# Decoder layer on one core: the modulation computed as rows on the tensor engine, and GpSimd's part of the mixer given to the vector engine

## The chip, the core and the metric

The kernel runs on one core of a Trainium2 chip. The metric is the device time of one execution in microseconds (us). The engines are TensorE (PE, with its weight loads PEld), VectorE (DVE), ScalarE (ACT), GpSimd (POOL) and SyncE (SP, which here issues nearly all loads).

## The reference, cut to what matters

One decoder layer on 256 tokens of width 1024. Six modulation vectors come from one condition vector; a mixer (block attention of 8 heads beside gated linear attention of 4 heads, merged by gates) is followed by a mixture of 32 experts, 4 per token.

```python
c_act = jax.nn.silu(c)                                   # (1, 1024)
mod = (c_act @ w_ada[l] + b_ada[l])[:, None, :]          # (1, 1, 6*1024)
shift1, scale1, gate1, shift2, scale2, gate2 = jnp.split(mod, 6, axis=-1)
h = _rmsnorm(x, norm1_w[l]) * (1.0 + scale1) + shift1
x = x + gate1 * _mixer(h, w_in[l], ...)
h = _rmsnorm(x, norm2_w[l]) * (1.0 + scale2) + shift2
x = x + gate2 * _moe(h, w_router[l], ...)
return _rmsnorm(x, final_norm_w)
```

All arrays are float32. `w_ada` is 1024 x 6144 (25 MB), `w_in` 1024 x 8208, the experts' weights 32 x 12.6 MB, some 403 MB.

## The kernel before, in words

The activations lie transposed: 128 partitions hold channels, the free dimension holds the 256 tokens. A unit is 256 channels, a tile of 128 x 2 x 256.

**Products in the mixer.** A product makes 256 output columns from 1024 inputs in four quarters, one for each unit of the input. Its weights are split into a rounded high part `wh` (`split_hi`, a ScalarE copy, L385) and a low part `wl` (`split_lo`, a subtraction, L389). A quarter is 12 matmuls in which the tile of weights or of activations is loaded and 256 columns stream (`quarter`, L403). Five pairs of split buffers are there. Which engine makes `wl` is written down: quarters 1 and 3 of a product on GpSimd, 0 and 2 on VectorE.

**First block.** The six products that gated linear attention needs first (q, k, half of v) run unit by unit over the input (j = 0 to 3, six quarters each), since a unit of the normalised input `h` exists only when its shift and scale do. `ada_block(j)` loads the two 256-column pieces of `w_ada` for unit j. `ada_steps` accumulates them on VectorE in eight steps of 128 x 512 (L356, L358), `norm_unit` sums over the partitions with four one-column matmuls (L501), adds the bias and makes `h` (L514 to L518).

**Other modulation.** The vectors 2 to 5 (gate1, shift2, scale2, gate2) come from `ada_chain`: eight VectorE steps of 128 x 1024 (L819, L821), two transposes and two sums (L829, L831), a small matmul (L836) and additions (L841). It is a background chain.

**Order.** Engines run their instructions in the order in which they were issued. Products are jobs in a list, and between half quarters `side` lets background chains (levels of the linear attention, its output, gates, rotation, attention heads, modulation) issue a step. It does so by a planner's estimate of each engine's time (`use("V", 0.61)` and the like), with limits on how far an engine may lag. Loads go through a ring of 80 KB per partition in a fixed order; the next load is issued when `used` has been called often enough on the oldest tile.

**Names of the background work.** `level` forms the decays of one distance in linear attention: differences (GpSimd L655, VectorE L656), exponential (L658), products (GpSimd L660, VectorE L661), a matmul (L667, L683). `gla_out` is its output (GpSimd L742 and L758), `rot` the rotation of queries and keys (VectorE L949, L950, GpSimd L952, VectorE L954), `attn` a head of attention (first matmul L893).

**Experts.** After the mixer the 32 experts run one after another; their loads come through the same ring and two more. Their two products stream 512 columns against weight tiles of 64 columns, two side by side (L1328, L1362).

Of the kernel before, what the change touches and what calls it, by code (L numbers as in the profile page):

```python
# [9 lines left out]
F32 = mybir.dt.float32  # L10
# [3 lines left out]
OP = mybir.AluOpType  # L14
# [18 lines left out]
AHEAD, BACKLOG, PLO = 4, 3.0, (1, 3)  # L33
# [13 lines left out]
M_MOD = M_SEG + 64  # L47
M_N = M_MOD + 128
# [10 lines left out]
def constants():  # L59
# [23 lines left out]
    m[:, M_MOD:M_MOD + 128] = (p[:, None] % 32) == (p[None, :] % 32)  # L83
# [20 lines left out]
def layer(ctx, tc, a, out, dbg=None):  # L104
# [51 lines left out]
    modT = const.tile([128, 6, 8], F32, name="modT")  # L156
    bc = [128, 2, NE]
# [15 lines left out]
    with ExitStack() as mx:  # L173
# [85 lines left out]
        def ada_block(j, i):  # L259
# [7 lines left out]
            return queue(emit, 4)  # L267

        def first_block(j, n0, n1):
            def emit():  # L270
                wa = ring.tile([128, 2, 2, 512], F32, name="w")
# [4 lines left out]
            return queue(emit, 2 * (n1 - n0))  # L276
# [3 lines left out]
        la, lw = [], []  # L280
        for j in range(4):
            la.append([ada_block(j, i) for i in range(2)])
            lw.append([first_block(j, 0, 2), first_block(j, 2, 3)])
        l_ada = {v: [] for v in range(2, 6)}

        def ada_loads(v, n):
            for _ in range(n):
                i = len(l_ada[v])
                l_ada[v].append(queue(lambda i=i: wtile(kview(w_ada, D * v, D * v + D, 2 * i, 2 * i + 2)), 2))
# [4 lines left out]
        for v, lst, c0 in ((4, l_gr, C_GR), (3, l_gb, C_GB), (2, l_ga, C_GA)):  # L294
            for i in range(2):
                lst.append(chunk(w_in, c0 + 512 * i))
                if v > 2:
                    ada_loads(v, 2)
        for u in range(4):
# [4 lines left out]
            ada_loads((2, 5)[u // 2], 2)  # L304
# [24 lines left out]
        for u in range(2):  # L329
            V.tensor_mul(sx[u], x0[u], x0[u])  # L330
            S.activation(sx[2 + u], x0[2 + u], AF.Square)
        V.tensor_tensor(sx[0], sx[0], sx[1], op=OP.add)
        V.tensor_mul(cact, cact, vec[:, R_C:R_C + 8])
        V.tensor_tensor(sx[0], sx[0], sx[2], op=OP.add)
# [3 lines left out]
        acc, tpa = {}, [Bank()]  # L338

        def ada_products(k):  # L340

            ld = la[0][k // 4]
            for v in range(2):
                for b in range(2):
                    i = 2 * v + b
                    PE.matmul(tpa[0].t[:, i:i + 1], ld.tv[:, k % 4, v, 128 * b:128 * b + 128], cact[:, k:k + 1],
                              start=(k + i == 0), stop=False, skip_group_check=True)
            ld.used()

        def ada_steps(j, ks, first=True):  # L350
            for k in ks:
# [1168 lines left out]
```

## Time and profile before

| what | value |
|---|---|
| median of 3 runs (lowest to highest) | 1349.86 us (1344.20 to 1350.17) |
| the profiled execution's own time | 1352.94 us |
| its span, first to last instruction | 1351.0 us |
| mean granted clock of TensorE | 0.972 |
| PE, DVE, ACT, POOL busy | 1221.2, 483.6, 290.7, 220.4 us |
| loaded and stored | 480.18 MB |

The span has five stretches, which the program's names mark off: the first block until 82 us; the rest of linear attention and the gates until 210; rotation and attention until 325; the merge and the output product until about 432, where the second expert's matmuls begin to follow each other; then the experts. Busy time of PE is no measure of progress here, since its matmuls overlap: the time from one start to the next is.

### The profile page before, as it was taken

To read this page: it belongs to the slowest core of one execution; us is meant where nothing else is said; L and a number is where in the kernel's file an instruction comes from. 1 tells how busy PE (TensorE), PEld (TensorE's weight loads), DVE (VectorE), ACT (ScalarE), POOL (GpSimd) and SP (SyncE) were. 2 spreads that over 40 slices of the span, in tenths; PEclk is the share of its full clock that TensorE was granted. 3 is DMA by queue.
4 is the path that set the end of the run, shared out by engine and by line. 5 is a ranking of instruction groups with operands and counts; after the bars stand their busy time and mean duration, and the time that the engine had idled before them with its cause. 6 is when DMAs were issued, how large, how long until landed. Compare 5 with 4: busy or idle time off the path is not lost.

```text
span 1351.0 us, 16184 instructions
## 1 busy us (share of the span) xinstructions
PE 1221.2 (90%) x6616; PEld 675.0 (50%) x6616; DVE 483.6 (36%) x800; ACT 290.7 (22%) x597; POOL 220.4 (16%) x153
## 2 busy tenths in 40 slices
PE   6797997879999989999999999898989889898986
PEld 5697997879985434434434333342433334242322
DVE  6749897878533121211221112111111121111112
ACT  3263655445432101101011010110101011010102
POOL 3656574554431000000000000000000000000000
PEclk9799799899999989999999999999999999999998
DMA  8997469567688999999999999999999999999993
GB/s 272 317 285 217 95 150 199 161 177 269 252 310 325 416 414 397 427 427 427 427 427 427 426 426 428 428 426 427 426 428 426 426 426 427 427 427 428 426 426 143
DMA packets 73292, 480.18 MB, mean 355 GB/s; under 512 B 7456, under 2 KB 23984, under 8 KB 48512
## 3 DMA queue, kind: packets, MB, share of 16 engines
q1 hardware_dynamic: 69808, 476.60, 90.2%
q10 hardware_dynamic: 3264, 2.23, 0.5%
q8 instruction: 53, 0.87, 0.3%
q0 software_dynamic: 144, 0.30, 0.1%
q14 instruction: 23, 0.19, 0.0%
HBM read 478.06 MB, written 1.05 MB: 355 GB/s over the span
## 4 chain that ended last, share of the span: by engine, by line
DMA 41%; PE 26%; DVE 1%; issue 0%; ACT 0%; SPq 0%; DVEq 0%; ACTq 0%
DMA w<-in_w_exp_in_dram 26%; DMA w<-in_w_exp_out_dram 15%; PE h L1328 13%; PE g L1362 7%; PE y L1372 2%; PE g L1262 1%; PE g L1352 1%; PE h L1320 1%; PE y L1238 0%; PE h L1218 0%; PE g L1251 0%; DVE o L1424 0%; PE g L1281 0%; DVE u L1366 0%; PE g L1218 0%
## 5 line engine op out<-in xcount | busy, mean ns | idle before, releaser
L1328 PE MATMUL h<-w,xg 128*64 128x512 f32 x2048 | 464.9, 599 | 23.1 <-DMA w<-in_w_exp_in_dram 23.1
L1328 PEld LDWEIGHTS h<-w,xg 128*64 128x64 f32 x2048 | 140.6, 137 | 306.1 <-issue 272.2
L1362 PE MATMUL g<-w,aT 128*64 128x512 f32 x1024 | 230.2, 599 | 28.0 <-DMA w<-in_w_exp_out_dram 14.7
L1341 DVE TENSOR_SCALAR sg<-h 128x512 f32<-128x512 f32 x32 | 22.1, 692 | 524.2 <-PE h L1328 514.3
L403 PE MATMUL ps_a<-m,wh 128*128 128x256 f32 x896 | 176.6, 298 | 3.1 <-ACT m L516 2.0
L389 POOL TENSOR_TENSOR wl<-w,wh 128x512 fp32r<-128x512 f32 x98 | 143.3, 1471 | 110.8 <-ACT wh L385 91.2
L1362 PEld LDWEIGHTS g<-w,aT 128*64 128x64 f32 x1024 | 72.8, 137 | 171.8 <-issue 147.3
L403 PEld LDWEIGHTS ps_a<-m,wh 128*128 128x128 f32 x896 | 148.1, 202 | 4.3 <-ACT m L516 2.1
L403 PE MATMUL ps_a<-m,wl 128*128 128x256 f32 x448 | 131.5, 294 | 12.4 <-DVE wl L389 12.4
L1354 ACT COPY aT<-g 128x512 f32<-128x512 f32 x32 | 18.7, 586 | 509.7 <-PE g L1352 509.7
L385 ACT CAST wh<-w 128x512 fp32r<-128x512 f32 x176 | 106.0, 616 | 97.0 <-PE ps_a L403 70.5
L1366 DVE TENSOR_TENSOR u<-g,u 64x512 f32<-64x512 f32 x64 | 44.0, 688 | 199.4 <-PE g L1362 198.7
L403 PEld LDWEIGHTS ps_a<-m,wl 128*128 128x128 f32 x448 | 90.1, 201 | 13.6 <-DVE wl L389 13.6
L389 DVE TENSOR_TENSOR wl<-w,wh 128x512 fp32r<-128x512 f32 x78 | 75.4, 969 | 23.4 <-ACT wh L385 23.4
L1342 ACT ACTIVATE sg<-sg 128x512 f32<-128x512 f32 x32 | 20.2, 631 | 189.8 <-DVE sg L1341 189.8
L1262 PE MATMUL g<-Psel,u 128*128 128x128 f32 x512 | 60.5, 276 | 0.0
L1372 PE MATMUL y<-u,pT 128*128 128x512 f32 x128 | 59.2, 605 | 0.8 <-DVE u L1366 0.8
L1262 PEld LDWEIGHTS g<-Psel,u 128*128 128x128 f32 x512 | 58.5, 192 | 0.1
L821 DVE SCALAR_TENSOR_TENSOR acc<-w,cact,acc 128x1024 f32<-128x1024 f32 x28 | 44.7, 1597 | 11.5 <-DMA w<-in_w_ada_dram 11.4
L1271 ACT ACTIVATE xg<-xg,shift 128x128 f32<-128x128 f32 x128 | 40.9, 390 | 27.7 <-DVE xg L1268 26.2
L1372 PEld LDWEIGHTS y<-u,pT 128*128 128x128 f32 x128 | 23.0, 189 | 36.8 <-issue 34.6
L403 PE MATMUL ps_a<-u,wh 128*128 128x256 f32 x224 | 40.5, 283 | 0.0
(302 smaller groups left out, 1071.0 us busy)
## 6 DMA issues: line engine op xcount, KB each, us to landing
w<-in_w_exp_in_dram SPq DMA_DIRECT2D x128, 2048.0 KB, 38.8
w<-in_w_exp_out_dram SPq DMA_DIRECT2D x63, 2048.0 KB, 38.1
w<-in_w_in_dram SPq DMA_DIRECT2D x26, 1024.0 KB, 10.4
w<-in_w_ada_dram SPq DMA_DIRECT2D x16, 1024.0 KB, 12.9
w<-in_w_ada_dram SPq DMA_DIRECT2D x32, 256.0 KB, 6.7
w<-in_w_in_dram SPq DMA_DIRECT2D x12, 512.0 KB, 7.3
w<-in_w_o_gla_dram SPq DMA_DIRECT2D x4, 1024.0 KB, 11.7
w<-in_w_o_moba_dram SPq DMA_DIRECT2D x4, 1024.0 KB, 11.7
```

The costliest lines, as they stand in the source:

```text
L385: S.copy(wh, wv)
L389: (G if pool_lo else V).tensor_tensor(wl, wv, wh.bitcast(F32), op=OP.subtract)
L403: PE.matmul(o, lhsT, rhs, start=(b + k + n == 0), stop=(k == 7 and n == 2), skip_group_check=True)
L821: V.scalar_tensor_tensor(acc_, w, ck, acc_, op0=OP.mult, op1=OP.add)
L1262: PE.matmul(o, flat(hx[t, q])[:, 128 * kk:128 * kk + 128], P[:, t], start=(n == 0), stop=(n == 3))
L1271: S.activation(xg[:, kk, 0:w_], xg[:, kk, 0:w_], AF.Identity, bias=shift2[:, kk:kk + 1])
L1328: PE.matmul(ph[64 * hf_:64 * hf_ + 64, 512 * b:512 * b + 512], xg[:, k, SL * i:SL * i + SL], wi[k // 2][:, k % 2, 1024 * hf_ + 512 * b:102 ...
L1341: V.tensor_scalar(sg_, ph[:, 0::2], LIMIT, None, op0=OP.min)
L1342: S.activation(sg_, sg_, AF.Sigmoid, scale=ALPHA)
L1362: PE.matmul(po[64 * n:64 * n + 64, :], aT[:, cc, 64 * hf_:64 * hf_ + 64], wo[hf_][:, cc, 512 * n:512 * n + 512], start=(hf_ + cc == 0), st ...
L1366: V.tensor_mul(flat(og[n])[64 * par:64 * par + 64], po[64 * n:64 * n + 64], flat(g2[n])[64 * n:64 * n + 64])
L1372: PE.matmul(y[t, n], pT[0:rows, 128 * t:128 * t + 128], flat(og[n])[0:rows], start=False, stop=True, skip_group_check=True)
```

## The change

- The modulation is computed on TensorE. The condition vector is the stationary operand, one column of it spread over 32 columns, and 512 columns of `w_ada` stream: `ada_rows(j)` makes 8 such matmuls per unit of the first block, `modulation(v)` 16 for each vector from 2 to 5. Four of them stand in the four 32-column parts of the array and write the four 32-partition parts of a bank. ScalarE copies the bank, and `turn_rows` turns rows into columns with four small matmuls, after which one VectorE addition gives the vector. `ada_steps`, `ada_products` and `ada_chain` are gone.
- `modulation` is a job between products, no background chain; its four loads come together in the ring's order.
- In the mixer all of GpSimd's arithmetic goes to VectorE: `split_lo`, the first halves in `level` (whose two differences become one instruction of 1024 columns, while the exponential becomes two of 512), sums and products in `gla_out`, the rotation, the scaling of x and the sums of squares.
- The sum of squares at the start goes through 16 one-column matmuls instead of VectorE additions and 2.
- The ring's order in the first block interleaves weights and modulation more finely, and the half-used weight tile gets half the room. The planner's prices change (0.53 to 0.63, 0.61 to 0.72, 0.65 to 0.73).

```diff
-        def ada_steps(j, ks, first=True):
-            for k in ks:
-                ld = la[j][k // 4]
-                w, ck = ld.tv[:, k % 4], cact[:, k:k + 1]
-                if first and k == ks[0]:
-                    acc[j] = unit()
-                    V.tensor_scalar(acc[j], w, ck, None, op0=OP.mult)
-                else:
-                    V.scalar_tensor_tensor(acc[j], w, ck, acc[j], op0=OP.mult, op1=OP.add)
-                ld.used()
+        def turn_rows(bk, ev, sel, n):
+            for c in range(4):
+                PE.matmul(bk[:, c:c + 4 * n:4] if n > 1 else bk[:, c:c + 1], ev[:, 128 * c:128 * c + 128], sel,
+                          start=True, stop=True, skip_group_check=True)
+        def ada_rows(j):
+            bk = Bank()
+            for i in range(2):
+                for k in range(4):
+                    PE.matmul(bk.t[32 * k:32 * k + 32, :], cact[:, 4 * i + k:4 * i + k + 1].to_broadcast([128, 32]),
+                              la[j][i].tv[:, k].rearrange("p v n -> p (v n)"), start=(i == 0), stop=(i == 1),
+                              skip_group_check=True)
+                la[j][i].used()
+            ev = unit()[:, :, 0:T].rearrange("p a b -> p (a b)")
+            S.copy(ev, bk.t)
+            return bk, ev
...
-        def split_lo(wv, wh, wl, pool_lo):
-            (G if pool_lo else V).tensor_tensor(wl, wv, wh.bitcast(F32), op=OP.subtract)
+        def split_lo(wv, wh, wl):
+            V.tensor_tensor(wl, wv, wh.bitcast(F32), op=OP.subtract)
...
+                if j < 3 and n == PNORM - 1:
+                    rows = ada_rows(j + 1)
                 if j < 3 and n == PNORM:
-                    norm_unit(j + 1)
+                    norm_unit(j + 1, rows)
...
+        def modulation(v):
+            def f():
+                bk = bank("a")
+                for i, ld in enumerate(l_ada[v]):
+                    for g in range(4):
+                        PE.matmul(bk[32 * g:32 * g + 32, :],
+                                  cact[:, 2 * i + g // 2:2 * i + g // 2 + 1].to_broadcast([128, 32]),
+                                  ld.tv[:, g // 2, 512 * (g % 2):512 * (g % 2) + 512], start=(i == 0), stop=(i == 3),
+                                  skip_group_check=True)
+                    ld.used()
+                ev = late.tile([128, 512], F32, name="ev")
+                S.copy(ev, bk)
...
+                    turn_rows(bk, ev, rows_[:, 1:3], 2)
+                    V.tensor_tensor(modT[:, v], bk[:, 0:8], vec[:, col:col + 8], op=OP.add)
...
-                yield {"V": 1.2}, "G"
-                G.tensor_tensor(sw, sw, sinb, op=OP.mult)
-                yield {"G": 1.25}, "V"
+                yield {"V": 1.4}, "V"
+                V.tensor_mul(sw, sw, sinb)
```

On TensorE at the start of the program the kernel before has this order: products of the condition with the first weights (L346), the sum of squares (L367), its spreading (L372), sums of the VectorE accumulator (L501), then the first quarter.

```order
L346 MATMUL ps_b<-cact,w 128x1 x4
L367 MATMUL y<-ones,u 128x1 x2
L372 MATMUL y<-kt,rs_171 128x128 x2
L346 MATMUL ps_b<-cact,w 128x1 x4
L501 MATMUL ps_b<-ones,u 128x1 x4
L403 MATMUL ps_a<-m,wh 128x256 x2
```

In the changed kernel the same place reads as follows; L353 is `ada_rows`, L345 `turn_rows`, L400 the quarter.

```order
L365 MATMUL ps_b<-ones,u 128x1 x16
L353 MATMUL y<-w,cact 32x512 x8
L371 MATMUL ps_b<-kt,rs_182 128x128 x2
L345 MATMUL y<-rows,u 128x1 x4
L400 MATMUL ps_a<-m,wh 128x256 x2
```

The matmuls with 512 streamed columns have come in ahead of the first quarter, and the sum of squares has grown from 2 to 16 matmuls.

On VectorE in the first block, from making unit 0 of the input (L514, L518) to making unit 1, the kernel before has the eight accumulation steps and no split.

```order
L514 TENSOR_SCALAR u<-u,s_170,modT 128x256 x2
L518 TENSOR_TENSOR m<-u,m 128x256 x2
L356 TENSOR_SCALAR u<-w,cact 128x512
L358 SCALAR_TENSOR_TENSOR u<-w,cact,u 128x512 x7
L504 TENSOR_TENSOR modT<-ps_b,vec 128x2x2
L507 SCALAR_TENSOR_TENSOR s_170<-modT,vec 128x2
```

In the changed kernel the same stretch (units are made by L508 and L512, x is scaled by L580) holds splits.

```order
L508 TENSOR_SCALAR u<-u,s_181,modT 128x256 x2
L512 TENSOR_TENSOR m<-u,m 128x256 x2
L386 TENSOR_TENSOR wl<-w,wh 128x512 x2
L580 TENSOR_TENSOR u<-u 128x512
L386 TENSOR_TENSOR wl<-w,wh 128x512
L498 TENSOR_TENSOR modT<-y,vec 128x2x2
L501 SCALAR_TENSOR_TENSOR s_181<-modT,vec 128x2
```

Eight steps that need the modulation's weights are gone from between the two units, and GpSimd's splits and its scaling of x stand there.

On VectorE in the attention stretch, around the rotation of the third pair of heads' queries, modulation steps (L821) stand between the parts of the rotation in the kernel before.

```order
L821 SCALAR_TENSOR_TENSOR acc<-w,cact,acc 128x1024
L949 STREAM_SHUFFLE rope<-q 32x512
L950 TENSOR_TENSOR q<-q,mt 32x512
L389 TENSOR_TENSOR wl<-w,wh 128x512
L821 SCALAR_TENSOR_TENSOR acc<-w,cact,acc 128x1024
L931 TENSOR_TENSOR u<-y,u 128x256 x2
L821 SCALAR_TENSOR_TENSOR acc<-w,cact,acc 128x1024
L954 TENSOR_TENSOR q<-q,rope 32x512
```

In the changed kernel L927, L928, L930 and L931 are the rotation, all on VectorE.

```order
L927 STREAM_SHUFFLE rope<-q 32x512
L928 TENSOR_TENSOR q<-q,mt 32x512
L386 TENSOR_TENSOR wl<-w,wh 128x512
L930 TENSOR_TENSOR rope<-rope,mt 32x512
L931 TENSOR_TENSOR q<-q,rope 32x512
L909 TENSOR_TENSOR u<-y,u 128x256 x2
```

The modulation steps are gone, and the multiplication that GpSimd made stands one split behind the first half of the rotation.

## Rows read from the trace of the kernel before

**Rows 1.** The page's chain that ended last: shares of the span by engine.

```profile
DMA 41%; PE 26%; DVE 1%; issue 0%; ACT 0%; SPq 0%; DVEq 0%; ACTq 0%
```

**Rows 2.** The same chain in order of time, where it leaves TensorE for the loads: start, length, what.

```profile
719.70 5.33 PE h L1328 x24
725.04 37.95 DMA w<-in_w_exp_in_dram
```

**Rows 3.** Busy time of each engine in the stretches: length, then PE, PEld, DVE, ACT, POOL busy (instructions), granted clock, busy share of the DMA engines, GB/s.

```profile
0.00:82.00 82.00, 59.91 (x365) 55.14 (x366) 52.42 (x71) 27.61 (x48) 42.53 (x34) 0.90 0.97 293
82.00:210.00 128.00, 112.85 (x846) 110.30 (x845) 112.39 (x118) 72.37 (x114) 78.60 (x52) 0.92 0.68 178
210.00:325.00 115.00, 93.74 (x685) 89.29 (x685) 91.85 (x151) 55.40 (x121) 60.42 (x33) 0.93 0.68 179
325.00:432.00 107.00, 103.83 (x784) 89.92 (x783) 49.44 (x104) 44.04 (x87) 38.27 (x34) 0.98 0.79 298
432.00:725.00 293.00, 288.72 (x1351) 113.23 (x1351) 60.35 (x128) 29.32 (x73) 0.57 (x1) 0.99 1.00 421
725.00:1351.00 626.00, 562.16 (x2592) 217.15 (x2592) 117.12 (x233) 61.98 (x156) 0.00 (x0) 0.99 0.97 412
```

**Rows 4.** Who waited for whom on TensorE, in the first three stretches one after another (one row, then four, then three): us in total, times, longest.

```profile
PE ps_b L501 <- DVE u L358: 9.0, 2, 6.3
...
PE ps_a L403 <- DVE wl L389: 5.0, 4, 1.8
PE y L683 <- DVE g L661: 4.3, 1, 4.3
PE y L667 <- DVE g L661: 3.4, 1, 3.4
PE ps_b L683 <- DVE g L661: 1.6, 1, 1.6
...
PE ps_a L403 <- DVE wl L389: 11.7, 4, 5.9
PE y L893 <- DVE k L954: 4.6, 2, 2.6
PE ps_b L893 <- DVE k L954: 3.6, 2, 2.2
```

**Rows 5.** TensorE in order of time in the first block: start, length, operation, the wait before it.

```profile
47.86 1.84 PE L501 MATMUL ps_b<-ones,u 128*128 128x1 f32 x8 [6.32 <-DVE u L358]
49.56 0.77 PE L403 MATMUL y<-wh,m 128*128 128x256 f32 x2
...
50.35 0.63 PE L403 MATMUL y<-wh,m 128*128 128x256 f32 x2
...
50.99 0.63 PE L403 MATMUL y<-wh,m 128*128 128x256 f32 x2
...
54.40 0.40 PE L403 MATMUL ps_a<-m,wh 128*128 128x256 f32 x2
...
54.76 0.40 PE L403 MATMUL ps_a<-m,wh 128*128 128x256 f32 x2
...
65.83 0.77 PE L403 MATMUL y<-wh,m 128*128 128x256 f32 x2
```

**Rows 6.** VectorE, ScalarE and the load queue in order of time in the first block, in that order: the accumulation for unit 3, the wait of a split for its weights, the issue of the last unit's loads.

```profile
52.17 11.81 DVE L358 SCALAR_TENSOR_TENSOR u<-w,cact,u 128x512 f32<-128x512 f32 x7
...
42.81 0.62 ACT L385 CAST wh<-w 128x512 fp32r<-128x512 f32 x1 [6.14 <-DMA w<-in_w_in_dram]
...
38.52 7.29 SPq L264 DMA_DIRECT2D w<-in_w_ada_dram  x8
46.24 1.87 SPq L273 DMA_DIRECT2D w<-in_w_in_dram  x3
```

**Rows 7.** Groups of instructions by line and shape on VectorE and then GpSimd, from 0 to 432 us: busy, mean ns of one, idle time before.

```profile
L389 DVE TENSOR_TENSOR wl<-w,wh 128x512 fp32r<-128x512 f32 x78 | 75.4, 969 | 23.4 <-ACT wh L385 23.4
L821 DVE SCALAR_TENSOR_TENSOR acc<-w,cact,acc 128x1024 f32<-128x1024 f32 x28 | 44.7, 1597 | 11.5 <-DMA w<-in_w_ada_dram 11.4
L358 DVE SCALAR_TENSOR_TENSOR u<-w,cact,u 128x512 f32<-128x512 f32 x26 | 31.3, 1206 | 2.4 <-DMA w<-in_w_ada_dram 1.6
...
L954 DVE TENSOR_TENSOR k<-k,rope 32x512 f32<-32x512 f32 x4 | 9.4, 2353 | 4.1 <-POOL rope L952 4.1
...
L993 DVE TENSOR_TENSOR gt<-ps_a,gt 128x512 f32<-128x512 f32 x4 | 2.8, 692 | 3.3 <-PE ps_a L403 3.3
...
L950 DVE TENSOR_TENSOR q<-q,mt 32x512 f32<-32x512 f32 x4 | 2.7, 679 | 0.1
...
L389 POOL TENSOR_TENSOR wl<-w,wh 128x512 fp32r<-128x512 f32 x98 | 143.3, 1471 | 110.8 <-ACT wh L385 91.2 <-issue 11.9 <-PE ps_a L403 7.1
L952 POOL TENSOR_TENSOR rope<-rope,mt 32x512 f32<-32x512 f32 x8 | 23.4, 2926 | 27.4 <-DVE rope L949 24.7 <-PE ps_a L403 2.7
```

**Rows 8.** VectorE in order of time in the attention stretch, where TensorE's longest wait for a split ends, and once more 56 us later.

```profile
233.33 1.29 DVE L821 SCALAR_TENSOR_TENSOR acc<-w,cact,acc 128x1024 f32<-128x1024 f32 x1 [5.82 <-DMA w<-in_w_ada_dram]
...
235.89 0.67 DVE L389 TENSOR_TENSOR wl<-w,wh 128x512 fp32r<-128x512 f32 x1
...
288.94 1.29 DVE L821 SCALAR_TENSOR_TENSOR acc<-w,cact,acc 128x1024 f32<-128x1024 f32 x1 [5.62 <-DMA w<-in_w_ada_dram]
```

**Rows 9.** TensorE in order of time among the first experts: tiles of 64 columns (L1328), transposes at the full array (L1352), full-width rows of 512 columns (L1238).

```profile
435.48 8.80 PE L1328 MATMUL h<-w,xg 128*64 128x512 f32 x40
444.21 0.75 PE L1352 MATMUL g<-kt,li 128*128 128x128 f32 x4
444.89 5.37 PE L1328 MATMUL h<-w,xg 128*64 128x512 f32 x24
...
461.74 3.70 PE L1238 MATMUL y<-u,wT 32*128 32x512 f32 x8
465.37 0.72 PE L1320 MATMUL h<-bx,sel 128*128 128x512 f32 x2
```

More of the change, by code (lines that the diff above doesn't have):

```diff
@@ L156, in layer @@
     modT = const.tile([128, 6, 8], F32, name="modT")
+    rows_ = const.tile([128, 3], F32, name="rows")
+    V.memset(rows_, 0.0)
+    for g in range(4):
+        V.memset(rows_[32 * g:32 * g + 1, 0:1], 1.0)
+        V.memset(rows_[32 * g:32 * g + 1, 1 + g % 2:2 + g % 2], 1.0)
     bc = [128, 2, NE]
@@ L266, in emit @@
                 return wa
-            return queue(emit, 4)
+            return queue(emit, 1)
         def first_block(j, n0, n1):
             def emit():
-                wa = ring.tile([128, 2, 2, 512], F32, name="w")
+                wa = ring.tile([128, n1 - n0, 2, 512], F32, name="w")
                 for n in range(n0, n1):
@@ L275, in emit, with ada_loads @@
                 return wa
-            return queue(emit, 2 * (n1 - n0))
+            return queue(emit, 2 * (n1 - n0), 4 * KB * (n1 - n0))
         blocks = [(C_GQ + 256 * u, False) for u in range(4)] + [(C_GV + 256 * u, True) for u in range(2)]
         nb_ = len(blocks)
-        la, lw = [], []
+        la, lw = [[ada_block(0, i) for i in range(2)]], []
         for j in range(4):
[L282 to L289, printed above, removed]
+            lw.append([first_block(j, 0, 2)])
+            if j < 3:
+                la.append([ada_block(j + 1, i) for i in range(2)])
+            lw[j].append(first_block(j, 2, 3))
+        l_ada = {}
+        def ada_loads(v):
+            l_ada[v] = [queue(lambda i=i: wtile(kview(w_ada, D * v, D * v + D, 2 * i, 2 * i + 2)), 1)
+                        for i in range(4)]
         l_gr, l_gb, l_ga, l_qk, l_v, l_og, l_om, l_ow = [], [], [], {}, {}, [], [], []
@@ L361, in layer @@
-        pn_ = Bank()
-        ada_products(0)
-        ada_steps(0, [1])
-        V.tensor_tensor(sx[0], sx[0], sx[3], op=OP.add)
-        V.tensor_tensor(sx[0][:, 0], sx[0][:, 0], sx[0][:, 1], op=OP.add)
-        for t in range(2):
-            PE.matmul(pn_.t[:, t:t + 1], sx[0][:, 0, 128 * t:128 * t + 128], ones[:, 0:1], start=True, stop=True)
+        def turn_rows(bk, ev, sel, n):
+            for c in range(4):
+                PE.matmul(bk[:, c:c + 4 * n:4] if n > 1 else bk[:, c:c + 1], ev[:, 128 * c:128 * c + 128], sel,
+                          start=True, stop=True, skip_group_check=True)
@@ L368, in layer @@
+        pn_ = Bank()
+        for u in range(4):
+            for b in range(2):
+                for t in range(2):
+                    PE.matmul(pn_.t[:, t:t + 1], sx[u][:, b, 128 * t:128 * t + 128], ones[:, 0:1],
+                              start=(u + b + t == 0), stop=(u + b == 4), skip_group_check=True)
         S.activation(rs1, pn_.t[:, 0:2], AF.Sqrt, bias=epst, scale=1.0 / D)
-        ada_steps(0, [3, 4], False)
+        rows0 = ada_rows(0)
         V.reciprocal(rs1, rs1)
@@ L494, in go, with norm_unit @@
             settle(True)
-        def norm_unit(j):
-            tp = Bank() if j else tpa[0]
-            for i in range(4):
-                cs = slice(128 * i, 128 * i + 128)
-                PE.matmul(tp.t[:, i:i + 1], flat(acc[j])[:, cs], ones[:, 0:1], start=(j + i > 0 and j > 0), stop=True,
-                          skip_group_check=True)
+        def norm_unit(j, rows):
+            tp, ev = rows
+            turn_rows(tp.t, ev, rows_[:, 0:1], 1)
             js = slice(2 * j, 2 * j + 2)
```

150 lines of the change are left out of this document (52 added, 98 removed).

## Prediction, made before the changed kernel ran

> **What bounds the kernel now.** I read the chain that ended last first [rows 1], then its order in time [rows 2]: from 725 us on it consists of expert loads alone, before that of the experts' matmuls. Then the stretches [rows 3]. From 432 us on the loads run at 421 and 412 GB/s with their engines 97 to 100% busy; the experts cannot run faster than that, whatever the mixer does. Before 432 us the loads run at 178 to 298 GB/s; they wait for room in the ring. So the span is the mixer's length plus a stretch that the loads fix, and a microsecond saved before 432 us is a microsecond at the end. I take that transfer as 1 to 1: the loads' shares from 432 us on (1.00, 0.97) leave nothing to be filled or lost there.
>
> What bounds the mixer? TensorE. A quarter's three matmuls take 0.36 us from start to start at the full clock (54.40 to 54.76) and 0.64 us at half of it (50.35 to 50.99) [rows 5]. The mixer has 38 products and the first block's 6, 176 quarters by the splits' counts, 78 on VectorE and 98 on GpSimd [rows 7], each of 12 matmuls: 176 x 4 x 0.36 = 253 us of 432. The rest is smaller matmuls, waits, and time at 1.2 instead of 2.4 GHz. Who ends the waits stands in [rows 4]; what the clock costs follows from the granted clock of a stretch [rows 3], since half the clock shows there as a loss of half the time: (1 - 0.90) x 82 = 8.2 us in the first, 0.08 x 128 = 10.2, 0.07 x 115 = 8.1 and 0.02 x 107 = 2.1 us. The engine had waited before these stretches (6.32 us ahead of 47.86, and the quarters after it run at the slow pace [rows 5]).
>
> **The price of the new matmuls.** No 32-column tile is in the trace. The nearest row is the experts' 64-column tiles: 40 records from 435.48 to 444.21, 0.218 us each [rows 9]. A full-width row of 512 columns costs 0.454 us per record (8 in 3.63 us) [rows 9]; two tiles side by side thus cost half of one. Each float32 matmul is two records (32 matmuls of an expert are the 64 records 40 + 24). If four tiles run beside each other as two do, a record is 0.109 us. The change has 4 x 8 + 4 x 16 = 96 such matmuls, 192 records: 21 us at 0.109, 42 us at 0.218, 87 us at 0.454. I take 0.109, since the step that the rows show, from one tile to two, is a clean halving; the other two are rivals. Turning rows into columns is 8 small records, 0.9 us at full clock by half of what L501's 8 cost at the slow one (1.70 us, 47.86 to 49.56 [rows 5]); in the first block they replace L501, behind it they are new.
>
> In the experts, four transposes between two runs of 64-column tiles take 0.68 us from first start to the next tile's (444.21 to 444.89), 0.17 us each [rows 9]; that is all a change of tile shape and back shows. The Trainium skill (TensorEngine Tiling (Array Packing), Tiling Modes, Key Properties) says that changing the tiling mode drains the engine. By that rule each of 16 changes would cost about 0.36 us (the last of 24 records takes 5.37 - 23 x 0.218 from its start to its end), an estimate of 6 us; but two changes and four transposes together take only 0.68 us here, so the trace shows no such cost, and the sum goes without it.
>
> **First block, 0 to 82 us.** Removed: TensorE's wait for the accumulation, 9.0 us [rows 4], and most of the slow clock that followed it, 6 of 8.2 us. Added: the rows of units 1 to 3, 16 records each, 3 x 1.75 = 5.2 us; at the start about 2 us, since the sum of squares is 28 records more at 0.21 us (6 us, half of it while x still arrives), and unit 0's rows go ahead of the first quarter while four splits stand on VectorE ahead of the unit's making. The floor is the loads: unit 3's modulation weights are issued until 45.8 us and the last weights until 48.1 [rows 6], with the engines' share at 0.97 [rows 3]; unit 2's split waited 6.14 us for its weights [rows 6]. Landing near 53 us puts unit 3's first quarter no earlier than about 57, against 65.83 now [rows 5]. So the block can give 9 + 2 = 11 us at most; by the engine's own sum 15 - 5.2 - 2 = 8. I take **-6.5 us** (-11 to 0), since the next block's loads begin no earlier.
>
> **Linear attention and gates, 82 to 210 us.** Waits: 5.0 us for splits, 9.3 for `level`'s products [rows 4], clock 10.2. VectorE is busy 112.4 of 128 us [rows 3], so its queue is long. Of it 24.9 us or more go with the modulation (28 steps of 1.6 us [rows 7], half of them here). Splits shrink from 0.97 us to the 0.69 that the same shape costs where GpSimd rests (L993) [rows 7], and all come to VectorE. I let 3.5 us of the splits' waits, 5 of `level`'s (its chain stays: difference, exponential, product) and 6 of the clock go: -14.5. Added: two modulations, 2 x (16 x 2 x 0.109 + 0.9) = 8.8. **-6 us** (-16 to +4).
>
> **Attention, 210 to 325 us.** Two waits of the splits are not VectorE's work but its queue: a modulation step stood 5.82 and 5.62 us for its weights [rows 8] with splits behind it; that is most of the 11.7 us [rows 4], and 10 of it go. The rotation runs VectorE, GpSimd, VectorE; GpSimd's part is 2.93 us and the addition behind it up to 2.35 [rows 7], against 0.68 each for the same shape uncontended (L950) [rows 7]. That is some 3 us less in each of 8 chains, and of the 8.2 us that TensorE waited for it [rows 4] 6 go. Of the clock's 8.1, 6 go. Added: two modulations, 8.8, less about 0.8 for the small matmuls dropped. **-14 us** (-20 to -4).
>
> **Merge, 325 to 432 us.** TensorE is busy 103.8 of 107 [rows 3]; GpSimd's splits here were ahead of need. **-1 us** (-4 to +1).
>
> **VectorE as a whole.** 306 us are busy before 432 [rows 3]. Gone: 76 us in L821 and L358 alone [rows 7]. Splits: 176 x 0.692 = 122 instead of 75.4, +46. GpSimd's others: 24 tiles of 512 columns (scaling, products, rotation, normalisation) at 0.69, 17 us, and a few small ones. Contention saves about 12 on L954 and its like. That is about 285 of some 405 us, 70% as now (306 of 432, 71%). On average it keeps up.
>
> **Sum.** -6.5 - 6 - 14 - 1 = -27.5 us. The profiled execution took 1352.94 us (its span 1351.0 and 1.9 around it), so it would be 1325.4; the median of the runs lies 3.1 us lower, at 1349.86, so the forecast is **1322 us**.
>
> **Rivals.**
> 1. *Nothing is left of the waits and the slow clock.* All lower ends: -51 us, 1299. For it: VectorE loses a fifth of its work at the crowded place, and a wait avoided also avoids the slow clock. Against: `level`'s chain of four engines stays.
> 2. *Tiles run in pairs only*, 0.218 us per record: +21 us, 1343.
> 3. *VectorE's order is the bound.* It now makes every split in program order, among `level`'s and the rotation's instructions; TensorE would wait for splits as now. Then only the first block (-6.5) and the two waits on modulation loads with their clock (-9.7 - 4) are won, and 16.8 us of modulation added behind the first block: -3.5, so 1346. For it: 88% busy from 82 to 210 us [rows 3]. Against: each split is a third shorter.
> 4. *Slower: the 32-column tiles run one after another*, each at the price of a full-width row, 0.454 us: 87 instead of 21 us, +66, so 1388. It decides from (27.5 + 21) / 192 = 0.25 us per record: above that the change loses. Against it: the 64-column tiles overlap.
>
> **How the numbers follow.** Chances: forecast 0.60 with a range of its own of 1306 to 1338, rival 1 0.10, rival 2 0.12, rival 3 0.12, rival 4 0.06. A measurement of this kernel tells about 0.5% (6.7 us, 1343.1 and 1356.6) from no change. Faster: 0.60 + 0.10 + half of rival 2 (0.06) + a little of rival 3 (0.02) = 0.78; same: 0.06 + 0.08 = 0.14; slower: rival 4 and a tail of rival 3, 0.08. The range goes from just below rival 1 to rivals 2 and 3, **1297 to 1345**; it leaves out rival 4, half of rival 3 and the far tail.
>
> **What would show it.** In the changed profile: records of the 32-column tiles about 0.11 us apart (L353, L809), 3.5 us per modulation; L389's successor L386 at about 0.69 us; unit 3's first quarter at 57 to 62 us; waits of TensorE before 432 us down from 54 us behind the start to some 25; granted clock of 0.95 or more from 82 to 325 us; the second expert's matmuls beginning near 405 us; loads saturated behind that as now. Wrong would be it if TensorE waits for splits by more than 15 us in all, if a modulation takes 7 us or more, if the first block still ends near 80 us because its loads come no earlier, or if the modulation job waits for its four loads.

## The result, and the profile after

The changed kernel takes **1300.54 us** (median of 4 runs, 1297.8 to 1304.11) against 1350.01 (4 runs of the kernel before): ratio 0.9644, 95% interval 0.9604 to 0.9684. The forecast was 1322, range 1297 to 1345. The profiled execution took 1304.11 us, its span is 1302.3.

Line numbers shift: the rows of the modulation are made in L353 (first block) and L809, turned into columns in L345; a split's low half is L386, the product of a quarter L400, a level's product L677, the rotation L927 to L932, the scores L871.

The stretches (the first four cuts at the same places of the program as in [rows 3], the last again where the chain that ended last leaves TensorE for the loads; length, PE, PEld, DVE, ACT, POOL busy with instructions, granted clock, DMA share, GB/s):

```profile
0.00:74.00 74.00, 64.67 (x442) 54.46 (x443) 29.61 (x73) 29.20 (x52) 2.27 (x6) 1.00 0.96 303
74.00:188.00 114.00, 113.38 (x936) 106.35 (x938) 85.60 (x137) 71.71 (x123) 0.00 (x0) 1.00 0.79 231
188.00:283.00 95.00, 94.24 (x767) 87.47 (x760) 70.20 (x155) 58.32 (x130) 0.00 (x0) 1.00 0.80 224
283.00:389.00 106.00, 102.79 (x766) 89.03 (x764) 58.59 (x126) 42.13 (x80) 4.81 (x6) 0.97 0.72 275
389.00:703.00 314.00, 309.77 (x1456) 122.86 (x1458) 66.38 (x141) 33.05 (x84) 0.57 (x1) 0.98 0.99 421
703.00:1302.30 599.30, 541.01 (x2490) 207.67 (x2486) 110.94 (x220) 58.30 (x145) 0.00 (x0) 0.99 0.97 415
```

From 74 to 283 us TensorE is busy for all but 1.4 us, at a granted clock of 1.00 where [rows 3] had 0.92 and 0.93. VectorE took over GpSimd's work and is nevertheless less busy: 244 us up to 389 instead of 306 up to 432. All that TensorE waited for from 30 to 389 us, to be laid beside [rows 4] (us in total, times, longest; the rows with 0.4 us or less left out):

```profile
PE ps_a L1145 <- DVE msk L1142: 1.3, 1, 1.3
PE ps_a L1013 <- DVE lbase L1010: 1.1, 1, 1.1
PE ps_a L345 <- ACT ev L815: 0.7, 1, 0.7
PE ps_a L400 <- DVE wl L386: 0.6, 1, 0.6
PE ps_a L1117 <- ACT m L1067: 0.5, 1, 0.5
```

The first two and the last are the router's and were there before. Of the waits for splits one of 0.6 us is left, those for the levels and for the rotation are gone, and from 74 to 283 us the granted clock is 1.00. The price of the new matmuls, TensorE in order of time: the turning of unit 3's rows with the quarter behind it, unit 3's own first quarter, and a whole modulation between two quarters.

```profile
59.04 0.95 PE L345 MATMUL y<-rows,u 128*128 128x1 f32 x8
59.84 0.48 PE L400 MATMUL y<-wh,m 128*128 128x256 f32 x2
...
62.80 0.40 PE L400 MATMUL ps_a<-m,wh 128*128 128x256 f32 x2
...
187.45 0.28 PE L400 MATMUL ps_a<-m,wl 128*128 128x256 f32 x1
187.66 3.64 PE L809 MATMUL ps_a<-w,cact 128*32 128x512 f32 x32
191.23 0.51 PE L400 MATMUL ps_a<-m,wh 128*128 128x256 f32 x2
```

From the first of the 32 records to the next quarter 3.57 us pass, 0.112 us per record; the change of tile shape and back is within that. Groups by line and shape, to be laid beside [rows 7]:

```profile
L386 DVE TENSOR_TENSOR wl<-w,wh 128x512 fp32r<-128x512 f32 x176 | 115.5, 684 | 38.6 <-ACT wh L382 37.9
...
L656 DVE TENSOR_TENSOR g<-g,gq 128x512 f32<-128x512 f32 x8 | 5.5, 685 | 0.0
L930 DVE TENSOR_TENSOR rope<-rope,mt 32x512 f32<-32x512 f32 x8 | 5.4, 672 | 0.0
```

The chain that ended last is as before [rows 1], loads and the experts' matmuls:

```profile
DMA 42%; PE 27%; DVE 1%; issue 0%; ACT 0%; SPq 0%; DVEq 0%; ACTq 0%
```

Where the 48.7 us between the two spans came from, by the same instruction in both traces: unit 3's first quarter 71.02 to 62.80 us (8.2); the last gate's activation 211.7 to 188.1 (15.4 more); the first product with `gt` 329.9 to 284.9 (21.4 more); the second expert's matmuls 435.5 to 392.4 (1.9 given back); the end (5.6 more). So 43 us come up to the second expert and 5.6 from the experts' stretch, which the forecast had left alone.

### The profile page after: what moved, and what is told of

The parts are those of the page before. It is cut to its first block, busy times and chain, and to the rows that moved or that the text cites. A ratio compares the mean times of both kernels' runs of the same rounds, so it can differ in the third digit from the quotient of the medians.

```text
span 1302.3 us, 16455 instructions
## 1 busy us (share of the span) xinstructions
PE 1225.9 (94%) x6844; PEld 667.8 (51%) x6844; DVE 421.3 (32%) x847; ACT 292.7 (22%) x612; POOL 7.6 (1%) x13
## 3 DMA queue, kind: packets, MB, share of 16 engines
HBM read 477.99 MB, written 1.05 MB: 368 GB/s over the span
## 4 chain that ended last, share of the span: by engine, by line
DMA 42%; PE 27%; DVE 1%; issue 0%; ACT 0%; SPq 0%; DVEq 0%; ACTq 0%
DMA w<-in_w_exp_in_dram 27%; DMA w<-in_w_exp_out_dram 15%; PE h L1305 14%; PE g L1339 7%; PE y L1349 2%; PE g L1239 2%; PE g L1329 1%; PE h L1297 1%; PE y L1215 0%; PE g L1228 0%; PE h L1195 0%; DVE o L1401 0%; PE g L1258 0%; DVE u L1343 0%; PE g L1195 0%
## 5 line engine op out<-in xcount | busy, mean ns | idle before, releaser
L400 PE MATMUL ps_a<-m,wh 128*128 128x256 f32 x896 | 172.0, 293 | 3.8 <-ACT m L510 3.8
L400 PEld LDWEIGHTS ps_a<-m,wh 128*128 128x128 f32 x896 | 144.0, 197 | 6.8 <-ACT m L510 3.8
L400 PE MATMUL ps_a<-m,wl 128*128 128x256 f32 x448 | 129.2, 288 | 0.6 <-DVE wl L386 0.6
L386 DVE TENSOR_TENSOR wl<-w,wh 128x512 fp32r<-128x512 f32 x176 | 115.5, 684 | 38.6 <-ACT wh L382 37.9
L400 PEld LDWEIGHTS ps_a<-m,wl 128*128 128x128 f32 x448 | 88.2, 197 | 0.8 <-DVE wl L386 0.8
L400 PE MATMUL ps_a<-u,wh 128*128 128x256 f32 x224 | 40.7, 283 | 0.0
L400 PE MATMUL ps_a<-wh,m 128*128 128x256 f32 x192 | 34.9, 284 | 0.0
L400 PEld LDWEIGHTS ps_a<-u,wh 128*128 128x128 f32 x224 | 34.4, 189 | 0.0
## 6 DMA issues: line engine op xcount, KB each, us to landing
w<-in_w_in_dram SPq DMA_DIRECT2D x26, 1024.0 KB, 14.3
```

The costliest lines, as they stand in the source:

```text
L386: V.tensor_tensor(wl, wv, wh.bitcast(F32), op=OP.subtract)
L400: PE.matmul(o, lhsT, rhs, start=(b + k + n == 0), stop=(k == 7 and n == 2), skip_group_check=True)
```

## The experiments

Two theories at the start. **Queue**: the gain comes from the modulation's leaving VectorE's order, where its steps stood for their loads with splits behind them [rows 8]. **Port**: it comes from GpSimd's leaving, since VectorE and GpSimd slow each other [rows 7]. All times below are medians; the kernel before took 1350.1 to 1350.3 beside these runs. Two smaller parts of the change, the finer order of the loads in the first block and the sum of squares on TensorE, were never run by themselves; every variant of the changed kernel keeps them. The places are starts in each run's trace: the last gate's activation, the first product with `gt`, the last merged unit `x1T`, the second expert.

| kernel | us | ratio to before (95%) | gate | gt | x1T | expert 2 |
|---|---|---|---|---|---|---|
| before | 1350.0 | | 211.7 | 329.9 | 404.1 | 435.5 |
| changed | 1300.5 | 0.9604 to 0.9684 | 188.1 | 284.9 | 361.0 | 392.4 |
| GpSimd back | 1324.3 | 0.9754 to 0.9850 | 199.6 | 304.8 | 377.5 | 413.6 |
| before, GpSimd moved | 1335.8 | 0.9842 to 0.9936 | 192.5 | 310.4 | 384.9 | 420.9 |
| tiles one by one | 1324.4 | 0.9755 to 0.9853 | 198.4 | 305.7 | 378.9 | 415.0 |
| GpSimd beside splits | 1368.7 | 1.0092 to 1.0185 | 214.7 | 338.9 | 428.7 | 464.7 |
| GpSimd on its own tile | 1306.3 | 0.9631 to 0.9715 | 191.6 | 289.2 | 363.2 | 399.3 |
| VectorE's time back | 1310.9 | 0.9669 to 0.9755 | 187.6 | 286.3 | 365.0 | 396.3 |
| GpSimd moved, waits only | 1319.0 | 0.9726 to 0.9826 | 184.5 | 295.4 | 369.9 | 401.2 |
| before, 32 bytes | 1340.7 | 0.9904 to 0.9985 | 204.8 | 323.3 | 397.5 | 428.9 |
| splits back | 1302.6 | 0.9627 to 0.9698 | 188.1 | 287.1 | 360.3 | 391.7 |
| chains back | 1313.8 | 0.9703 to 0.9775 | 196.7 | 293.5 | 369.6 | 400.9 |
| changed, aligned | 1298.3 | 0.9592 to 0.9648 | 187.9 | 284.8 | 360.8 | 392.2 |

**GpSimd back.** The changed kernel with GpSimd's part of the mixer returned to it:

```diff
-            V.tensor_tensor(wl, wv, wh.bitcast(F32), op=OP.subtract)
+            (G if pool_lo else V).tensor_tensor(wl, wv, wh.bitcast(F32), op=OP.subtract)
...
-                V.tensor_mul(sw, sw, sinb)
+                G.tensor_tensor(sw, sw, sinb, op=OP.mult)
```

> The changed kernel with all of GpSimd's work in the mixer put back on GpSimd (low halves of quarters 1 and 3, the normed units, two steps of each level of linear attention, the halves' sums, gv's scaling, the sine product of the rotation), with the planner's old prices for it; the modulation stays on TensorE. Queue theory (the gain comes from the modulation's leaving VectorE's in-order queue): at most 10 us over the changed kernel's 1300.5, about 1305, PE's idle time before 389 us still under 25 us. Port theory (the gain comes from GpSimd's leaving, since VectorE and GpSimd slow each other): most of the 49 us is gone, 1335 or more, and VectorE's splits cost 0.97 us again instead of 0.68.

1324.3, in the gap: 23.8 us lost where the queue theory allowed 10 and the port theory wanted 35. VectorE's splits took 0.86 us, not the 0.97 of the port theory. TensorE's waits there:

```profile
PE y L871 <- DVE k L932: 4.7, 3, 2.1
PE y L677 <- DVE g L655: 3.6, 4, 1.4
PE y L661 <- DVE g L655: 2.7, 1, 2.7
```

They are at the scores and at the levels, none at a split. Neither half of the change is enough.

**Before, GpSimd moved.** The kernel before with `V.` for `G.` at GpSimd's instructions of the mixer, same places, same prices.

> The kernel before with all of GpSimd's instructions in the mixer issued on VectorE at the same places of the program; the modulation stays on VectorE, the planner's prices stay. Queue theory: VectorE keeps the modulation's waits and gets 116 us more beside it, so that nothing is won: 1345 to 1365. Port theory: splits at about 0.69 us and no detours over a second engine, about 1310 to 1320.

1335.8, between the two ranges again: 14.3 us won beside 1350.1, so the port theory's half exists, but by itself it is the smaller one. At the last `x1T` the two halves win 26.6 (404.1 to 377.5) and 19.2 us (404.1 to 384.9), together 45.8, and the whole change 43.1: nearly the same sum, but not by adding up place by place. In the first block either half wins all there is (the first copy of `gv` starts at 70.4 and 70.8 us, 71.3 in the changed kernel, 79.6 before), and GpSimd moved does so without the new order of the loads; behind it the halves win 17.4 and 10.4 us, the whole 34.8. There each half leaves waits that the other would have removed (12.3 us at the levels and the scores with GpSimd back, 21.9 us for splits here).

**Tiles one by one.**

```diff
-                for i, ld in enumerate(l_ada[v]):
-                    for g in range(4):
+                for g in range(4):
+                    for i, ld in enumerate(l_ada[v]):
```

> The changed kernel with the modulation's matmuls reordered so that those of one tile of 32 columns follow each other (two in a row in the first block's row, four in a row for the later quarters), and not one of each tile in turn. If the four tiles work side by side and TensorE sets the mixer's pace: a record costs up to the 0.454 us of a full matmul instead of 0.118, 192 of them add up to 64 us, 1330 to 1365. If the low price comes from the 32 columns alone and not from neighbours in other tiles: 1300 to 1305.

1324.4, between the two ranges. TensorE in order of time in this kernel: a row of the first block and the quarter behind it, then a modulation of 32 records and the quarter behind it. Below that, weight loads of the same modulation, of which each record has one at its start:

```profile
55.49 1.94 PE L353 MATMUL y<-w,cact 128*32 128x512 f32 x16
57.36 0.50 PE L401 MATMUL y<-m,wh 128*128 128x256 f32 x2
...
159.85 8.86 PE L810 MATMUL ps_a<-w,cact 128*32 128x512 f32 x32
168.64 0.51 PE L401 MATMUL ps_a<-m,wh 128*128 128x256 f32 x2
```
```profile
160.30 0.11 PEld L810 LDWEIGHTS ps_a<-w,cact 128*32 128x32 f32 x1 [0.32 <-issue]
160.73 0.11 PEld L810 LDWEIGHTS ps_a<-w,cact 128*32 128x32 f32 x1 [0.32 <-issue]
161.16 0.11 PEld L810 LDWEIGHTS ps_a<-w,cact 128*32 128x32 f32 x1 [0.32 <-issue]
```

From the first record of the modulation to the quarter 8.79 us pass, 0.275 us per record instead of 0.112: the low price does come from the neighbours in the other tiles. The 0.275 is a mean of two kinds. The first records follow each other at 0.43 us, nearly the 0.454 of a full row [rows 9]; later, 12 of the 32 start within 0.03 us of the one before them (the trace doesn't name a record's tile). In the first block, where only two matmuls in a row go to one tile, nothing is lost: 1.87 us for 16 records, 0.117 each. 128 x (0.275 - 0.112) = 21 us of TensorE's time more make the first product with `gt` 20.8 us later and `x1T` 17.9; the missing 3 us are the slow clock of the changed kernel there (granted 0.97 from 283 on, 0.03 x 106 = 3.2), which doesn't occur in this run ahead of `x1T` (1.00). So TensorE's time is the mixer's time, nearly 1 to 1.

**GpSimd beside splits, and on its own tile.** Useless GpSimd work in the changed kernel, first on the split's halves, then on a private tile:

```diff
             V.tensor_tensor(wl, wv, wh.bitcast(F32), op=OP.subtract)
+            for b in range(2):
+                G.tensor_tensor(gd, wl[:, b].bitcast(F32), wh[:, b].bitcast(F32), op=OP.subtract)
```
```diff
             V.tensor_tensor(wl, wv, wh.bitcast(F32), op=OP.subtract)
+            G.tensor_copy(gs, wl[:, 0, 0:1].bitcast(F32))
+            G.tensor_tensor(gd, gd, gd, op=OP.subtract)
```

> The changed kernel with useless work on GpSimd beside each split: two subtractions of 128x256 that read the split's halves and write a tile that nobody reads (about 176 x 1.6 us of GpSimd); nothing waits for them but the split buffer's next use. Port theory: VectorE's splits go back to about 0.97 us and the time rises by 15 us or more, to 1315 to 1335. Queue theory: splits may get dearer, but VectorE is only 60 per cent busy, so the time rises by at most 5 us, to 1300 to 1306.

> The changed kernel with useless work on GpSimd beside each split that touches a tile of its own (one subtraction of 128x256 on a private tile, behind a copy of one column of the split's low half, which sets its moment): about 176 x 1.1 us, as much GpSimd time as the variant with GpSimd's work put back had (200 us). Nothing of the kernel's work runs on GpSimd. Theory that VectorE and GpSimd slow each other: the splits rise from 0.68 to 0.85 us or more, and the time rises by 8 to 25 us, to 1309 to 1325. Theory that GpSimd's own slowness on the path is what costs (its splits of 1.4 us, the hops to it and back): splits may rise, but the time stays within 5 us, 1298 to 1306.

The first came out at 1368.7, far above what either theory gave, and doesn't separate them. The splits rose to 1.01 us as the port theory wanted, but GpSimd was so slow (two times 0.97 us) that ScalarE stood for split buffers which GpSimd still read (who waited for whom on ScalarE):

```profile
ACT wh L382 <- POOL gd L390: 86.4, 65, 3.2
```

In the second nothing waits so. VectorE's and GpSimd's groups:

```profile
L390 DVE TENSOR_TENSOR wl<-w,wh 128x512 fp32r<-128x512 f32 x176 | 125.2, 741 | 31.8 <-ACT wh L382 22.2 <-POOL gd L392 4.5 <-DMA w<-in_w_ada_dram 3.5
...
L392 POOL TENSOR_TENSOR gd<-gd 128x256 f32<-128x256 f32 x176 | 138.5, 787 | 0.0
```

The splits rise only to 0.74 us, and the last `x1T` comes 2.2 us later. The time, 1306.3, is 5.8 us above the changed kernel's; the two intervals overlap, though no run of the one lies within the runs of the other, and in the profiled execution 4.7 us of the difference fall behind `x1T` (the last section). Slowing VectorE's splits by a tenth costs little, then; but the load on it was also weaker than in the kernel before, where a split took 0.97 us. The next two runs settle this.

**Splits back, chains back.** The two kinds of GpSimd's work returned one at a time, with the lines of the first diff above.

> The changed kernel with only the splits' low halves put back on GpSimd (quarters 1 and 3 of each product, and all but one in the first block), at the planner's old prices; the chains (levels of linear attention, sums, gv's scaling, rotation) stay on VectorE. Of the 16.5 us that the whole of GpSimd's work put back cost up to the end of the mixer (last x1T at 377.5 us instead of 361.0): theory that the splits on GpSimd are what costs, 10 us or more here, 1311 or more. Theory that the chains on GpSimd cost (each level and each rotation waits for a slower step there): at most 5 us here, 1298 to 1307.

> The changed kernel with only the chains put back on GpSimd (two steps of each level of linear attention, the halves' sums, gv's scaling, the sine product of the rotation, the normed units), the splits all on VectorE. Theory of the chains: 10 us or more, 1311 or more, with PE's waits at the levels' matmuls and at the scores as in the run with all of it put back. Theory of the splits: at most 5 us, 1298 to 1307.

With the splits back (groups on VectorE and GpSimd):

```profile
L386 DVE TENSOR_TENSOR wl<-w,wh 128x512 fp32r<-128x512 f32 x78 | 66.4, 853 | 31.5 <-ACT wh L382 31.5
...
L386 POOL TENSOR_TENSOR wl<-w,wh 128x512 fp32r<-128x512 f32 x98 | 136.9, 1402 | 212.7 <-ACT wh L382 191.7 <-PE ps_a L400 13.9 <-DVE sm L888 3.4
```

VectorE's splits are slowed to 0.85 us, GpSimd's take 1.40, and nothing is lost: 1302.6, `x1T` at 360.3. The splits stand four quarters ahead of their use. With the chains back it is 1313.8, `x1T` 8.6 us later: TensorE waits at the levels again (4.1 us), and its first quarter starts at 25.7 instead of 22.7 us. The first four splits on VectorE, which stand ahead of the making of unit 0, show why; first in the changed kernel, then with the chains back, where GpSimd scales x at the same time:

```profile
19.21 2.50 DVE L386 TENSOR_TENSOR wl<-w,wh 128x512 fp32r<-128x512 f32 x4 [0.66 <-ACT wh L382]
```
```profile
17.73 5.82 POOL L580 TENSOR_TENSOR u<-u 128x512 f32<-128x512 f32 x4 [14.41 <-ACT u L374]
18.99 5.71 DVE L386 TENSOR_TENSOR wl<-w,wh 128x512 fp32r<-128x512 f32 x4 [5.86 <-ACT wh L382]
```

Three of the splits take 1.74 to 1.77 us beside GpSimd, and the fourth 0.68 once GpSimd is done. So the port theory falls as it was put: the engines do slow each other, but for the splits that stand ahead of their use it costs nothing. It costs where the slowed step stands in a chain that TensorE waits for, as here at the start (3.0 of the 8.6 us). Both kinds back cost 16.5 at `x1T`, more than 8.6: VectorE's product in the levels takes 1.45 us there and 1.05 with the chains alone. How much of that difference is the slowing and how much GpSimd's own order, where a chain's step then stands among splits of 1.4 us, no run separates.

The Trainium skill (SBUF — State Buffer, Terms) says that VectorE and GpSimd share a port pair that one of them holds for a whole instruction while the other stands. The durations agree in direction: 0.68 to 0.85 us in the mean for a split beside 98 GpSimd instructions of 1.4 us, and 1.74 to 1.77 us for the three splits above.

**VectorE's time back, and GpSimd moved with waits only.** What of the modulation's steps was the cost on VectorE? The first adds their time without their loads to the changed kernel, the second takes their time out of "before, GpSimd moved" and leaves their waits (four of the six modulation vectors come out incomplete in it, so the experts' work behind them can differ):

```diff
+                        V.scalar_tensor_tensor(acc_, acc_, cact[:, i:i + 1], acc_, op0=OP.mult, op1=OP.add)
+                    yield {"V": 1.2}, ""
```
```diff
-                    V.scalar_tensor_tensor(acc_, w, ck, acc_, op0=OP.mult, op1=OP.add)
+                    V.scalar_tensor_tensor(acc_[:, 0:1], w[:, 0:1], ck, acc_[:, 0:1], op0=OP.mult, op1=OP.add)
```

> The changed kernel with as much useless work on VectorE as the modulation's steps of the later quarters were (28 steps of 128x1024 and 16 of 128x512 on a private tile, put in line by the planner at the old price), without any wait for a load. Theory that VectorE's time was the cost of the modulation there: the time rises by 12 us or more, to 1312 to 1325. Theory that the steps' waits for their loads, with the splits behind them, were the cost: at most 5 us more, 1298 to 1306.

> The kernel before with GpSimd's instructions on VectorE, as in the run before, but 28 of the 32 steps of the later quarters' modulation take one column instead of 1024 (so four of the six modulation quarters come out incomplete): each still waits for its load in VectorE's queue, at the same place, and costs next to nothing else. Theory that VectorE's time was the cost: 10 to 25 us under the 1336 of the run with the whole steps, 1311 to 1326. Theory that the waits for loads were the cost: within 6 us of it, 1330 to 1338.

The first gave 1310.9 (`x1T` 4.0 us later), between the two bounds: VectorE's time alone costs something, but less than the theory of time said (part of it may be the order, since the planner places what it prices). The second gave 1319.0, 16.8 us under the whole steps, as that theory said; 15.0 of it are there at `x1T`, ahead of the choice of experts. So the steps' time weighs most where waits stand in the same queue; that a wait leaves a backlog which long steps prolong is my reading of the two, not measured by itself. What the waits do by themselves is seen in this second run, VectorE and then TensorE in order of time:

```profile
195.61 0.67 DVE L389 TENSOR_TENSOR wl<-w,wh 128x512 fp32r<-128x512 f32 x1
207.74 0.22 DVE L821 SCALAR_TENSOR_TENSOR acc<-w,cact,acc 128x1 f32<-128x1 f32 x1 [11.46 <-DMA w<-in_w_ada_dram]
207.88 0.69 DVE L389 TENSOR_TENSOR wl<-w,wh 128x512 fp32r<-128x512 f32 x1
```
```profile
208.62 0.58 PE L403 MATMUL ps_a<-wl,m 128*128 128x256 f32 x1 [7.28 <-DVE wl L389]
209.00 0.63 PE L403 MATMUL ps_a<-wh,m 128*128 128x256 f32 x2
```

A step of one column waits 11.46 us for its load; the split behind it is next; TensorE stands 7.28 us for that split and then goes on at half pace (0.64 us from 209.00 to the next three matmuls at 209.64, against 0.36 [rows 5]). All its waits for splits there sum to 19.0 us. In the changed kernel no matmul waits for these loads: TensorE is idle for 0.0 us ahead of L809.

**Before, 32 bytes; changed, aligned.** The 5.6 us of the experts' stretch: the landings of the experts' loads (2 MB each) follow each other in 4.90 us (median for each of nine buffers, 600 to 1250 us) before, and after in 4.84 to 4.85 for the five buffers of the first ring, 4.88 for one and 4.90 for three. The change adds a small tile (`rows`) ahead of that ring, so its start moves by 32 bytes (as reckoned from the sizes of the tiles, from 32 short of a multiple of 4096 onto one; no trace shows an address). The three at 4.90 are those of a ring allocated from the other end, which did not move.

```diff
     modT = const.tile([128, 6, 8], F32, name="modT")
+    pad = const.tile([128, 8], F32, name="pad")
+    V.memset(pad, 0.0)
```

> The kernel before with an unused tile of 32 bytes a partition among the constants, so that the ring that the experts' loads land in starts at the same place as in the changed kernel (a multiple of 4096 bytes instead of 32 bytes short of one); nothing else changes. If the place in memory explains that the experts' loads of 2 MB land every 4.84 us instead of every 4.90 in the changed kernel, in those buffers that moved and in no other: the same here, 430 GB/s instead of 427 in the experts' stretch, and 3 to 6 us less than before, about 1345. If the rate comes from anything else in the change: 427 GB/s and 1350.

> The changed kernel with two unused tiles (480 bytes at the far edge, 128 bytes in the experts' pool), which move the four of the nine buffers of the experts' loads that don't lie on a multiple of 512 bytes onto one; nothing else changes. If the place sets the rate: all nine at 4.84 us per load instead of 4.88 to 4.90 in those four, 434 GB/s instead of 430, and 190 loads bring 4 to 5 us, about 1296. Otherwise 430 GB/s and 1300.5.

The experts' stretch (columns as above) of before, before with 32 bytes, changed, changed and aligned:

```profile
600.00:1250.00 650.00, 604.68 (x2808) 232.82 (x2808) 122.00 (x247) 60.68 (x155) 0.00 (x0) 1.00 1.01 427
```
```profile
600.00:1250.00 650.00, 611.14 (x2848) 237.22 (x2849) 124.20 (x252) 63.82 (x163) 0.00 (x0) 0.99 1.01 430
```
```profile
600.00:1250.00 650.00, 604.38 (x2812) 232.12 (x2813) 123.95 (x248) 61.87 (x156) 0.00 (x0) 1.00 1.01 430
```
```profile
600.00:1250.00 650.00, 605.80 (x2813) 233.09 (x2810) 123.93 (x248) 61.27 (x155) 0.00 (x0) 1.00 1.01 430
```

The unused 32 bytes alone bring 430 GB/s and 1340.7 us (0.9904 to 0.9985 of before). Of its 9.6 us some 6 are the rate, 0.7% of the 919 us behind 432 us in which the loads bound [rows 3]; the rest isn't explained by it, as its mixer also ran 6.6 us shorter in the one trace, and runs of the kernel before spread over 14 us. All traces agree on the direction: from the second expert to the end the three kernels with the old place (before; GpSimd moved; waits only) take 913 to 916 us, the ten with the new one 903 to 910. The second kernel did not do what I expected: all nine buffers now land every 4.85 us, but the rate stays at 430, and 1298.3 can't be told from 1300.5. It is the lowest median of all, and no proven gain. In its one trace the stretch from the second expert to the end is 6.7 us shorter than in the changed kernel's (903.3 against 909.9), but the rate between 600 and 1250 us doesn't show from where. What the last buffers bring stays open.

## Why the prediction was right, and where its sizes were off

The direction, the bound and the mechanism were right; the forecast was 21 us too high, and the time is close to rival 1 (1299).

1. *TensorE sets the mixer's time, 1 to 1*: right, by the tiles one by one (21 us more of TensorE's time, 20.8 us later at the first product with `gt`).
2. *0.109 us per record of a 32-column tile*: 0.112. Turning took 0.95 us, as forecast. Rival 2 (0.218) and rival 4 (0.454) fall. A record with none beside it does cost nearly what rival 4 said (0.43 in the tiles one by one), but even that kernel won (1324.4): the 128 records of its later modulations take 0.275 in the mean and the first block's 0.117, some 0.23 together, just under the 0.25 from which rival 4 saw a loss. That point also hung on the gain, which I had too small.
3. *Changes of tile shape cost nothing*: right, 3.57 us for 32 records with both changes in it. By the Trainium skill's rule (TensorEngine Tiling (Array Packing), Tiling Modes, Key Properties: a change of mode drains the engine) the estimate was 6 us in all; the trace doesn't show it.
4. *First block, -6.5*: -8.2, within its bounds. The row at 65.83 us [rows 5] that I took for unit 3's first quarter is unit 2's fifth; it is at 59.84 now, within the 57 to 62 named. Unit 3's own went from 71.02 to 62.80. The start cost more than the 2 us of the sum: the first quarter begins at 22.7 instead of 19.2 us.
5. *Linear attention and gates, -6*: **-15.4**. The term that failed is what I kept of the waits: 1.5 us of the splits', 4.3 of `level`'s ("its chain stays"), 4.2 of the clock's, 10 us in all. All of it went but 0.6 us. The chain did stay, but its price was VectorE's and GpSimd's steps (for `g` x `gq` 1.36 us before, 1.45 with GpSimd back, 1.05 with the chains alone back, 0.685 now).
6. *Attention, -14*: **-21.4**, beyond its lower end of -20. Again the remainder was counted as staying: 1.7 us for splits, 2.2 for the rotation, 2.1 of the clock, 6 us; it went too.
7. *Merge, -1*: +1.9, past its end of +1: the clock fell there once (0.97), which cost 3.2 us.
8. *The loads saturated behind that as now*: saturated they were (0.99 and 0.97), but no term had that their rate could change: -5.6 us, most of it from the place of a ring in memory, as the kernel before with 32 bytes more shows.
9. *Waits of TensorE down from 54 to some 25 us*: to about 5 from 30 to 389 us (48 before, from 30 to 432). With the waits the slow clock went too, from 0.92 and 0.93 to 1.00 between the first block and the merge; the rows show the half pace right behind a long wait (6.32 us in [rows 5], 7.28 in the waits only). The two were sized apart, each with a remainder, and went as one.
10. *VectorE 70% busy*: 63% (244 of 389). I took the lesser contention to save 12 us, on the rotation and its like; other instructions got shorter too (`g` x `gq` by half).
11. *Rival 3, VectorE's order is the bound*: 0.6 us of waits for splits. What had made splits late was steps waiting for loads ahead of them, not their number: with all splits on VectorE and waits alone left of the steps, 19.0 us of such waits remain.

The whole ran close to rival 1's 1299 by another sum than its lower ends: the first block and the merge came out later than there, and 5.6 us came from the loads.

## What to carry to other kernels

An instruction that waits for a load belongs on an engine whose order can afford it: in a queue that others depend on, its wait and everything behind it are charged to the bound engine, and the slow clock after that once more. Of work on a slower engine, what stands ahead of its use was free here, even where it slowed a neighbour; what is a step of a chain, or slows one, wasn't, so move the chains first. Where waits and clock loss come together, size them as one term that goes or stays whole.

## What the runs showed of the hardware that was not expected

- **Moving a load's buffers by 32 bytes changes its rate**: 4.90 us per 2 MB before, 4.84 to 4.85 in the same five buffers after; 427 against 430 GB/s over the stretch. Which boundary matters isn't shown.
- **The order of the matmuls decides what 32-column tiles save**: a record with none beside it takes 0.43 us, in turn over four tiles it is 0.112 and with two matmuls in a row to a tile 0.117, but with four in a row 0.275.
- **VectorE and GpSimd slow each other by more than the means tell**: a split on VectorE takes 0.68 us alone and 1.74 to 1.77 beside GpSimd at work without a gap.
- **The granted clock makes 4.7 us of difference in one place.** From the last `x1T` to the second expert the instructions are the same in all kernels (the router, with waits of 1.1, 0.5 and 1.3 us in the changed one), yet it takes 31.3 us in some and 36.0 to 36.1 in others. The changed kernel and GpSimd back:

```profile
361.00:392.40 31.40, 28.55 (x177) 16.78 (x175) 12.53 (x40) 9.94 (x22) 4.81 (x6) 1.00 0.77 300
```
```profile
377.50:413.60 36.10, 33.25 (x176) 20.43 (x175) 11.96 (x40) 9.87 (x22) 4.79 (x6) 0.86 0.72 279
```

  The granted clock was 1.00 in the one and fell to 1.2 GHz for a part of the other (0.86). With one trace per kernel it isn't shown whether the kernel, the chip or chance decides (all four traces taken on one chip have the longer time, and one of the others). Differences under 5 us between two of these kernels were therefore read at the last `x1T`, ahead of this place.
